# Loads of the down-weight blocks separated from their sums, in the first token group of a one-core encoder layer

## The chip, the cores and the metric

The kernel runs as one program on one core of a Trainium2 chip. The metric is the device time of one execution in microseconds (us). Before the change the median of 3 runs is 2419.88 us (2419.79 to 2422.89). The core's engines are called as in the profile: PE multiplies matrices into PSUM, PEld is its weight load, DVE, ACT and POOL work element by element, SP only issues DMA transfers. Each engine takes its instructions in the order of its own queue and waits at the head of it.

## The reference

The reference computes one layer of a streaming encoder on 2048 prompt frames and 64 sample frames, 1024 wide: RMSNorm, a combined input projection, three mixers (RG-LRU, multi-scale pooling, stick-breaking attention), an output projection, and then the part that matters here, the feed-forward block:

```
h2 = rms_norm(x, lw["ffn_norm"])
ff = jax.nn.silu(h2 @ lw["w_gate"]) * (h2 @ lw["w_up"])
x = x + ff @ lw["w_down"]
```

`w_gate` and `w_up` are 1024 x 2816, `w_down` is 2816 x 1024, all in float32.

## The kernel before

The mixers take the first 990 us or so; the feed-forward block takes the rest. Its 2112 tokens are cut into three groups of 704 columns (`GT`), each group into two halves of 352 (`HT`). The 2816 hidden units are cut into 11 pairs (p = 0 to 10) of two blocks of 128. Every float32 operand is split into a rounded high part and a low rest, and three matmuls (high by high, high by low, low by high) make one product.

The gate and up projections of a pair (`gate`, `up`) are done by `seven`: a 2 x 2 block product made of seven products instead of eight, from sums of weight blocks and sums of token blocks. One product is 12 matmuls into one of five PSUM banks called `gu`; DVE combines the banks (L1185 makes `u`, L1213 and L1236 add for the gate and the up half, L1237 multiplies gate by up), and a bank is free when its last reader is done.

In the first group the sums of gate and up weights are made on DVE (L1130, L1131, L1132, L1137), used, and written to DRAM (`wsc`) for the two groups after it. The down projection of the first group is plain: `DN(p)` loads four blocks of `w_dn` (L1271), splits them, and makes 16 results of 6 matmuls, each in one of three PSUM banks called `dn`; DVE adds each to the accumulator `acc` (L1285), which frees its bank.

Two side jobs run in the first group, for the later groups. `H2_sums` makes the token sums of the next group from `x1all` (L1154 loads, L1155 to L1161 compute, L1163 stores to `hsc`); it runs in pairs 1, 3, 5 and 7. `D_sums(p)` loads the four blocks of pair p's down weights (L1292, two transfers of 512 KB), makes four sums of them on DVE (L1294 to L1297, each 128 x 512, in place) and stores them to DRAM (`wsd`, L1299). Both jobs share two staging buffers, `xh` and `xg`, one of each, handed out in turn by `hstage()`. So a load into a staging buffer waits until the stores of the job before it have landed, and it waits at the head of SP's queue, with the other loads and stores behind it.

Where L1294 to L1297 work: the two loads fill `st[0]` and `st[1]`; L1294 reads and writes `st[1]` alone, L1295 and L1296 read both. In most pairs `st[0]` is `xh` and `st[1]` is `xg`.

What sets the order: the kernel is written as one program, but a scheduler of the framework places each engine's instructions before the launch, from its own estimate of when each will be ready (`schedule_with_timeline_sim=True`), and where two are ready it takes the one that is written earlier. So the side jobs stand in the queues where their buffers and data are expected to be ready, not where they are written. In the kernel before, all 11 `D_sums` stand within the work of the first five pairs of the first group.

Of the kernel before, what the change touches and what calls it, by code (L numbers as in the profile page):

```python
# [31 lines left out]
NF = FF // P  # L32
# [17 lines left out]
def hybrid_layer(ctx: ExitStack, tc: tile.TileContext, x_all, x_t, w_in, w_out, w_gu, w_dn, par, gates, poolw,  # L50
# [161 lines left out]
    def stage():  # L212
        return ws.tile([P, 1024], F32, name="stg", tag="stg", bufs=prm("b_st", 2))
# [752 lines left out]
    for k in range(KD):  # L966
        st = stage()
# [82 lines left out]
    def H2_row(gi):  # L1050
        rb = pr2.tile([P, GT], F32, name="rb2")
        sp.dma_start(rb, x1row[0:1, gi * GT:(gi + 1) * GT].to_broadcast([P, GT]))
        return rb
# [46 lines left out]
    def ps_gu():  # L1100
        return psF.tile([P, 512], F32, name="gu", tag="gu", bufs=5)
# [44 lines left out]
    def hstage():  # L1146
        flop[0] ^= 1
        return pr2.tile([P, 2, GT], F32, name="xh") if flop[0] else pf.tile([P, 2, GT], F32, name="xg")

    def H2_sums(gi, k, rb):  # L1150

        xh, tt = hstage(), hstage().rearrange("p a t -> p (a t)").rearrange("p (b t) -> p b t", b=4)
        for e in range(2):
            sp.dma_start(xh[:, e, :], x1all[k + 4 * e][:, gi * GT:(gi + 1) * GT])  # L1154
            dve.scalar_tensor_tensor(xh[:, e, :], xh[:, e, :], gn2_sb[:, k + 4 * e:k + 4 * e + 1], rb, ALU.mult, ALU.mult)  # L1155
        b11, b12, b21, b22 = xh[:, 0, :HT], xh[:, 0, HT:], xh[:, 1, :HT], xh[:, 1, HT:]
        t1, t2, t3, t4 = (tt[:, i, :] for i in range(4))
        dve.tensor_tensor(t1, b12, b11, ALU.subtract)
        dve.tensor_tensor(t3, b22, b12, ALU.subtract)
        dve.tensor_tensor(t2, b22, t1, ALU.subtract)  # L1160
        dve.tensor_tensor(t4, b21, t2, ALU.subtract)  # L1161
        for n, t in (("b11", b11), ("b21", b21), ("b22", b22), ("t1", t1), ("t2", t2), ("t3", t3), ("t4", t4)):
            sp.dma_start(hsc[gi][n][:, k, :], t)  # L1163

    def H2_load(gi, n, hl=None):
        st = hstage().rearrange("p a t -> p (a t)").rearrange("p (k t) -> p k t", k=4)
        sp.dma_start(st, hsc[gi][n])
        h, l = HB[n] if hl is None else hl
        act.copy(h, st)
        (gp if BL.index(n) % 2 else dve).tensor_tensor(l, st, h, ALU.subtract)  # L1170
# [37 lines left out]
    def gate(gi, p):  # L1208
        s = [pf.tile([P, GT], F32, name="s", bufs=4) for _ in range(2)]

        def use(i, x, y):
            o = s[i // 2][:, (i % 2) * HT:(i % 2) * HT + HT]
            dve.tensor_tensor(o, x, y, ALU.add)  # L1213
            act.activation(o, o, AF.Silu)

        seven(wsum(gi, p, 0), use)
        return s

    def up(gi, p, s):
        res = []  # L1220
        if gi:
            tt = pb.tile([P, 4, HT], F32, name="tt", bufs=1)
            t1, t2, t3, t4 = (tt[:, i, :] for i in range(4))
            b11, b12, b21, b22 = s[0][:, :HT], s[0][:, HT:], s[1][:, :HT], s[1][:, HT:]
        else:
            for e in range(2):
                res.append((pg.tile([P, GT], F32R, name="ah", bufs=2), pg.tile([P, GT], F32R, name="al", bufs=2)))

        def keep(b, t):
            sp.dma_start(asc[gi][p][b], t)  # L1230

        def use(i, x, y):
            cs = slice((i % 2) * HT, (i % 2) * HT + HT)
            o = s[i // 2][:, cs]
            v = tmp("v", 2)
            dve.tensor_tensor(v, x, y, ALU.add)  # L1236
            dve.tensor_tensor(o, o, v, ALU.mult)  # L1237
            if gi == 0:
                ah, al = res[i // 2]
                act.copy(ah[:, cs], o)  # L1240
                dve.tensor_tensor(al[:, cs], o, ah[:, cs], ALU.subtract)  # L1241
            elif i == 0:
                keep("b11", b11)
            elif i == 3:
                keep("b22", b22)
            elif i == 1:
                dve.tensor_tensor(t1, b12, b11, ALU.subtract)
                dve.tensor_tensor(t2, b22, t1, ALU.subtract)
                dve.tensor_tensor(t3, b22, b12, ALU.subtract)
                for b, t in (("t2", t2), ("t1", t1), ("t3", t3)):  # L1250
                    keep(b, t)
            else:
                dve.tensor_tensor(t4, b21, t2, ALU.subtract)
                keep("b21", b21)
                keep("t4", t4)

        seven(wsum(gi, p, 1), use)
        acts[p] = res
# [6 lines left out]
    def DN(p, extra=()):  # L1265
        extra = list(extra)
        for half in range(2):
            w = pg.tile([P, 2, 1024], F32R, name="wd", bufs=2)
            for q in range(2):
                r = raw()  # L1270
                sp.dma_start(r, w_dn[(2 * p + q) * P:(2 * p + q + 1) * P, half * 512:half * 512 + 512])  # L1271
                qs = slice(q * 512, q * 512 + 512)
                act.copy(w[:, 0, qs], r)
                rest(w[:, 1, qs], w[:, 0, qs], r)
            w = w.rearrange("p s (q e) -> p s q e", q=2)
            for d in range(4 * half, 4 * half + 4):
                if extra:
                    extra.pop(0)()
                cs = slice((d % 4) * P, (d % 4) * P + P)
                for (a, b) in ((0, HT), (HT, GT)):  # L1280
                    ps = psF.tile([P, 512], F32, name="dn", tag="dn", bufs=3)
                    for q in range(2):
                        ah, al = acts[p][q]
                        mm3(ps[:, :HT], w[:, 0, q, cs], w[:, 1, q, cs], ah[:, a:b], al[:, a:b], q == 0, q == 1)
                    dve.tensor_tensor(acc[:, d, a:b], ps[:, :HT], acc[:, d, a:b], ALU.add)  # L1285
                if p == NF // 2 - 1:
                    sp.dma_start(y[d][:, :GT], acc[:, d, :])
    def D_sums(p):

        st = [hstage().rearrange("p a t -> p (a t)")[:, :1024].rearrange("p (q e) -> p q e", q=2) for _ in range(2)]  # L1290
        for half in range(2):
            sp.dma_start(st[half], w_dn[2 * p * P:(2 * p + 2) * P, half * 512:half * 512 + 512].rearrange("(q p) e -> p q e", p=P))  # L1292
        a11, a12, a21, a22 = st[0][:, 0], st[0][:, 1], st[1][:, 0], st[1][:, 1]
        dve.tensor_tensor(a22, a21, a22, ALU.add)  # L1294
        dve.tensor_tensor(a21, a11, a21, ALU.subtract)  # L1295
        dve.tensor_tensor(a11, a22, a11, ALU.subtract)  # L1296
        dve.tensor_tensor(a12, a12, a11, ALU.subtract)  # L1297
        for i, t in enumerate((a11, a22, a21, a12)):
            sp.dma_start(wsd[p][:, i, :], t)  # L1299

    for p in range(NF // 2):
        s = gate(0, p)
        while pend:
            pend.pop(0)(ps_gu(), pr2)
        if p:
            DN(p - 1)
        up(0, p, s)
        if p == 0:
            sp.dma_start(acc, x1all[:, :, :GT].rearrange("k p t -> p k t"))
        if p in (1, 3, 5, 7):  # L1310
            if p == 1:
                rb2 = H2_row(1)
            H2_sums(1, p // 2, rb2)
        D_sums(p)
    DN(NF // 2 - 1, [lambda n=n: H2_load(1, n) for n in BL])
    s_g0.close()

# [11 lines left out]
    for gi in (1, 2):  # L1331
        for p in range(NF // 2):
            s = gate(gi, p)
            up(gi, p, s)
            if gi == 1:
                if p in (1, 3, 5, 7):
                    if p == 1:
                        rb2 = H2_row(2)
                    H2_sums(2, p // 2, rb2)
                if p == 8:  # L1340
                    for n in BL[:3]:
                        H2_load(2, n, HB2[n])
                if p == NF // 2 - 1:
                    HB.update(HB2)
                    for n in BL[3:]:
                        H2_load(2, n)
# [163 lines left out]
```

## Time and profile before

| what | value |
|---|---|
| median of 3 runs | 2419.88 us |
| profiled execution | 2420.12 us |
| its span, first to last instruction | 2418.3 us |
| PE busy | 2282.5 us (94%) |
| DVE busy | 1564.8 us (65%) |
| ACT, POOL busy | 984.6 us (41%), 1120.0 us (46%) |
| DMA queue's packets | 63.7% of 16 engines' span |
| mean granted TensorE clock | 0.969 |

A row of a timeline has the start in us from the span's start, the duration, the engine (SPq is SP's DMA queue), the line, the operation, output and input tiles, how many instructions are merged, and in brackets the engine's idle time before it and what ended that. A row of waits has the engine and line that waited, what released it, the total in us, how often, and the longest. Rows of windows have the busy time and instruction count of each engine, the granted clock (1.00 is full speed), the share of DMA engine time, and GB/s.

### The profile page before, as it was taken

Reading aid. Unit: us, or ns where it says so; the run is one execution under the profiler, and the core shown is the slowest. Engines: PE = TensorE matmul, PEld = TensorE weight load, DVE = VectorE, ACT = ScalarE, POOL = GpSimd, SP = SyncE. Lnnn points to the kernel's source line nnn. Section 1 sums busy time; section 2 is a strip of 40 time slices with the busy share of each in tenths; the row PEclk is TensorE's granted clock in tenths of the full one; section 3 lists DMA queues with packets and bytes.
Section 4 is the critical chain, followed back from the end, with each engine's and each line's share of the span. In section 5 each row is a group of like instructions: output and inputs, shape, how many; then the busy total and the mean of one; then the engine's idle time right before and its main releaser. Section 6 shows DMA issues by size and latency. Waiting matters only on the chain.

```text
span 2418.3 us, 38959 instructions
## 1 busy us (share of the span) xinstructions
PE 2282.5 (94%) x13966; PEld 2170.3 (90%) x13966; DVE 1564.8 (65%) x2371; ACT 984.6 (41%) x1790; POOL 1120.0 (46%) x807
## 2 busy tenths in 40 slices
PE   6988999999989989988899999999999999999999
PEld 5886878779779989888899999999999999999999
DVE  4568485795798643587767767776556665544554
ACT  4535364464565422332233334244444434333332
POOL 3534031130131133564556658487677677744442
PEclk8999999999999989999999999999999999999999
DMA  8986777666545354677764435976656666665664
GB/s 273 265 282 204 229 219 225 196 200 197 179 155 160 104 151 124 230 242 250 241 212 117 141 114 185 298 237 185 190 181 195 196 189 207 185 184 157 213 213 141
DMA packets 288260, 475.65 MB, mean 197 GB/s; under 512 B 44226, under 2 KB 153603, under 8 KB 280131
## 3 DMA queue, kind: packets, MB, share of 16 engines
q1 hardware_dynamic: 288066, 473.16, 63.7%
q8 instruction: 111, 1.82, 0.3%
q14 instruction: 83, 0.67, 0.1%
HBM read 337.22 MB, written 135.82 MB: 196 GB/s over the span
## 4 chain that ended last, share of the span: by engine, by line
PE 64%; DVE 14%; DMA 14%; issue 3%; ACT 2%; SPq 1%; POOL 1%; DVEq 0%; ACTq 0%; POOLq 0%
PE gu L78 37%; PE mm L78 13%; PE dn L78 10%; PE z L78 2%; PE av L78 2%; DVE C L665 2%; DMA x<-in_w_gu 1%; PE tp L709 1%; DVE xc L537 1%; DMA rbk<-row 1%; DMA rb<-xrow 1%; DVE s L1237 1%; DMA K<-kscr 1%; DMA xg<-in_w_dn 1%; DMA x1all<-xr 1%
## 5 line engine op out<-in xcount | busy, mean ns | idle before, releaser
L86 POOL TENSOR_TENSOR w<-x,w 128x512 fp32r<-128x512 f32 x539 | 773.5, 1448 | 525.6 <-ACT w L1108 482.3
L78 PE MATMUL gu<-ht,w 128*128 128x352 f32 x2131 | 543.3, 326 | 14.6 <-ACT w L1108 5.7
L1108 ACT CAST w<-x 128x512 fp32r<-128x512 f32 x539 | 328.0, 618 | 415.5 <-PE gu L78 261.6
L78 PE MATMUL mm<-hTh,w 128*128 128x512 f32 (+3 forms) x1632 | 433.1, 343 | 13.8 <-DVE xr L1009 8.5
L78 PE MATMUL gu<-hb,w 128*128 128x352 f32 x1622 | 407.1, 324 | 7.3 <-ACT w L1108 4.6
L78 PEld LDWEIGHTS gu<-ht,w 128*128 128x128 f32 x2131 | 379.6, 190 | 17.8 <-ACT w L1108 9.1
L78 PE MATMUL gu<-lt,w 128*128 128x352 f32 x1163 | 356.9, 325 | 0.0
L78 PEld LDWEIGHTS mm<-hTh,w 128*128 128x128 f32 x1632 | 292.0, 195 | 43.7 <-DVE xr L1009 9.5
L78 PEld LDWEIGHTS gu<-hb,w 128*128 128x128 f32 x1622 | 286.3, 189 | 9.0 <-ACT w L1108 5.4
L78 PE MATMUL mm<-hTl,w 128*128 128x512 f32 (+3 forms) x816 | 278.8, 342 | 1.4 <-POOL hTl L307 1.0
L78 PE MATMUL gu<-lb,w 128*128 128x352 f32 x991 | 279.3, 324 | 0.0
L78 PE MATMUL dn<-ah,wd 128*128 128x352 f32 x704 | 193.6, 333 | 26.1 <-DVE acc L1285 23.1
L78 PEld LDWEIGHTS gu<-lt,w 128*128 128x128 f32 x1163 | 217.5, 190 | 0.0
L78 PEld LDWEIGHTS gu<-lb,w 128*128 128x128 f32 x991 | 180.6, 190 | 0.0
L78 PEld LDWEIGHTS mm<-hTl,w 128*128 128x128 f32 x816 | 158.7, 195 | 16.1 <-POOL hTl L307 1.4
L665 DVE TENSOR_TENSOR_SCAN C<-z,C,zero 128x512 f32<-128x512 f32 (+4 forms) x148 | 160.5, 1087 | 13.2 <-ACT z L657 6.7
L78 PEld LDWEIGHTS dn<-ah,wd 128*128 128x128 f32 x704 | 130.2, 195 | 29.7 <-DVE acc L1285 26.0
L1237 DVE TENSOR_TENSOR s<-s,v 128x352 f32<-128x352 f32 x132 | 143.2, 1087 | 2.5
L1185 DVE TENSOR_TENSOR u<-gu,u 128x352 f32<-128x352 f32 x132 | 68.6, 520 | 81.1 <-PE gu L78 80.0
L78 PE MATMUL z<-K,q 128*128 128x512 f32 (+4 forms) x328 | 102.5, 396 | 18.3 <-DVE C L665 8.4
L574 POOL TENSOR_TENSOR i<-i,xc 128x512 f32<-128x512 f32 (+1 forms) x16 | 27.3, 1709 | 198.1 <-ACT i L562 146.9
L78 PE MATMUL dn<-al,wd 128*128 128x352 f32 x352 | 116.8, 332 | 0.4 <-DVE al L1241 0.4
(318 smaller groups left out, 4284.5 us busy)
## 6 DMA issues: line engine op xcount, KB each, us to landing
x<-in_w_gu SPq DMA_DIRECT2D x220, 256.0 KB, 3.9
w<-wk SPq DMA_DIRECT2D x46, 1024.0 KB, 6.1
x<-wsc SPq DMA_DIRECT2D x176, 256.0 KB, 4.1
wsc<-x SPq DMA_DIRECT2D x88, 256.0 KB, 3.9
x<-in_w_dn SPq DMA_DIRECT2D x77, 256.0 KB, 3.9
wk<-w SPq DMA_DIRECT2D x16, 1024.0 KB, 9.4
x<-wsd SPq DMA_DIRECT2D x44, 256.0 KB, 4.0
V<-vscr SPq DMA_DIRECT2D x40, 256.0 KB, 3.9
```

The source lines that it names most:

```text
L78: pe.matmul(out, lhsT, rhs, start=start, stop=stop)
L86: gp.tensor_tensor(out, src, hi, ALU.subtract)
L537: dve.scalar_tensor_tensor(xc[:, a:b], xa[:, s + j:s + j + b - a], pv("cw", c * 4 + j), xc[:, a:b], ALU.mult, ALU.add)
L574: gp.tensor_tensor(i, i, xc, ALU.mult)
L665: dve.tensor_tensor_scan(C[:n, :w][:, ::-1], om[:n, :w][:, ::-1], zero1[:n].to_broadcast([n, w]), carry, ALU.mult, ALU.add)
L709: pe.transpose(tp[:, kt, :], at[:, kt * P:(kt + 1) * P], ident)
L1108: act.copy(w[:, 0, :], src)
L1185: add = lambda o, x, y: dve.tensor_tensor(o, x, y, ALU.add)
L1237: dve.tensor_tensor(o, o, v, ALU.mult)
```

## The change

`D_sums` is cut in two. `D_load(p)` takes the two staging buffers and issues the two loads; `D_sums()` makes the sums and stores of the pair that was loaded last. In the first group `D_load(p)` stands at the end of pair p, and its sums at the end of pair p + 1, ahead of `H2_sums` and of the next `D_load`. The load of the last pair (p = 10) stands after the last `DN` with its loads of token sums, and its sums after `up` of the first pair of the second group. Nothing that is computed changes. In the changed program the loads are L1294, the four sums L1301 to L1304, the stores L1306.

```diff
+    dst_ = []
+
+    def D_load(p):
         st = [hstage()... for _ in range(2)]
         for half in range(2):
             sp.dma_start(st[half], w_dn[...])
+        dst_.append((p, st))
+
+    def D_sums():
+        p, st = dst_.pop(0)
         a11, a12, a21, a22 = st[0][:, 0], st[0][:, 1], st[1][:, 0], st[1][:, 1]
...
+        if p:
+            D_sums()
         if p in (1, 3, 5, 7):
             if p == 1:
                 rb2 = H2_row(1)
             H2_sums(1, p // 2, rb2)
-        D_sums(p)
+        if p < NF // 2 - 1:
+            D_load(p)
     DN(NF // 2 - 1, [lambda n=n: H2_load(1, n) for n in BL])
     s_g0.close()
+    D_load(NF // 2 - 1)
...
             up(gi, p, s)
             if gi == 1:
+                if p == 0:
+                    D_sums()
```

First place, SP's queue, around the load of pair 2 (`wsd_130` is the scratch of pair 0, so `wsd_131` and `wsd_132` are those of pairs 1 and 2; `wsc` stores and L1116 loads belong to gate and up weights). Before:

```order
L1292 DMA xg<-in_w_dn 128x2x512
L1141 DMA wsc_1_111<-x_10883 128x512
L1299 DMA wsd_131<-xh 128x512
L1141 DMA wsc_1_111<-x_10881 128x512
L1299 DMA wsd_132<-xg 128x512
L1292 DMA xh<-in_w_dn 128x2x512
L1141 DMA wsc_1_111<-x_10887 128x512
L1116 DMA x_11076<-in_w_gu 128x512
```

And now:

```order
L1306 DMA wsd_131<-xg 128x512
L1141 DMA wsc_1_111<-x_10875 128x512
L1306 DMA wsd_131<-xh 128x512
L1141 DMA wsc_1_111<-x_10873 128x512
L1294 DMA xg<-in_w_dn 128x2x512
L1294 DMA xh<-in_w_dn 128x2x512
L1141 DMA wsc_1_111<-x_10879 128x512
L1116 DMA x_11068<-in_w_gu 128x512
L1306 DMA wsd_132<-xg 128x512
```

The two loads of pair 2 now stand together; before, the second stood behind a store of pair 2's own first sum, and that sum waits for the first load. The second of the two stores of pair 1 out of `xg` now stands nearer to the first load.

Second place, DVE's queue, around the sums of pair 7, at the end of the down projection and in the up projection of pair 3. Before:

```order
L1185 TENSOR_TENSOR u_11927<-gu,u_11894 128x352
L1185 TENSOR_TENSOR u_11894<-gu,u_11894 128x352
L1236 TENSOR_TENSOR v<-gu,u_11927 128x352
L1285 TENSOR_TENSOR acc<-dn,acc 128x352
L1237 TENSOR_TENSOR s<-s,v 128x352
L1285 TENSOR_TENSOR acc<-dn,acc 128x352
L1294 TENSOR_TENSOR xg<-xg 128x512
L1285 TENSOR_TENSOR acc<-dn,acc 128x352
L1295 TENSOR_TENSOR xg<-xh,xg 128x512
```

And now:

```order
L1185 TENSOR_TENSOR u_11919<-gu,u_11886 128x352
L1285 TENSOR_TENSOR acc<-dn,acc 128x352
L1301 TENSOR_TENSOR xg<-xg 128x512
L1285 TENSOR_TENSOR acc<-dn,acc 128x352
L1302 TENSOR_TENSOR xg<-xh,xg 128x512
L1285 TENSOR_TENSOR acc<-dn,acc 128x352
L1185 TENSOR_TENSOR u_11886<-gu,u_11886 128x352
L1236 TENSOR_TENSOR v<-gu,u_11919 128x352
L1303 TENSOR_TENSOR xh<-xg,xh 128x512
```

The first sum of pair 7 now stands ahead of the second L1185 and of the first L1236 of that up projection; before it stood behind both.

Third place, DVE's queue, in the last down projection of the first group and the first pair of the second. Before:

```order
L1170 TENSOR_TENSOR lt_9625<-xh,ht_9624 128x1408
L1285 TENSOR_TENSOR acc<-dn,acc 128x352 x3
L1155 SCALAR_TENSOR_TENSOR xg<-xg,gn_sb,rb_16087 128x704
L1213 TENSOR_TENSOR s<-gu,c_15550 128x352
L1155 SCALAR_TENSOR_TENSOR xg<-xg,gn_sb,rb_16087 128x704
L1158 TENSOR_TENSOR xh<-xg 128x352
L1185 TENSOR_TENSOR u_15582<-gu,u_15552 128x352
```

And now:

```order
L1170 TENSOR_TENSOR lt_9625<-xh,ht_9624 128x1408
L1285 TENSOR_TENSOR acc<-dn,acc 128x352 x3
L1213 TENSOR_TENSOR s<-gu,c_15542 128x352
L1301 TENSOR_TENSOR xh<-xh 128x512
L1185 TENSOR_TENSOR u_15574<-gu,u_15544 128x352
L1302 TENSOR_TENSOR xg<-xh,xg 128x512
L1285 TENSOR_TENSOR acc<-dn,acc 128x352
L1303 TENSOR_TENSOR xg<-xh,xg 128x512
L1285 TENSOR_TENSOR acc<-dn,acc 128x352
L1304 TENSOR_TENSOR xg<-xg 128x512
```

The sums of pair 10 stand here now; the token sums of the third group (L1155 onward), which stood here, come about a dozen rows later. Elsewhere the sums of pairs 0 to 9 stand within a few rows of where they stood, still within the first five pairs of the first group: those of pair 6 three rows earlier (ahead of an L1132, an L1213 and an L1185), those of pair 9 ahead of the first L1285 of their down projection instead of behind it.

## Rows read from the trace of the kernel before

**Rows 1.** Windows of the first group: PE, PEld, DVE, ACT, POOL, clock, DMA, GB/s.
```profile
1060.00:1240.00 180.00, 154.91 (x898) 151.72 (x897) 133.98 (x215) 50.93 (x97) 90.44 (x65) 0.92 0.76 246
1240.00:1420.00 180.00, 180.00 (x1128) 180.00 (x1128) 127.80 (x199) 62.26 (x121) 109.23 (x78) 1.00 0.45 132
1100.00:1120.00 20.00, 13.21 (x59) 12.46 (x58) 12.99 (x22) 4.75 (x10) 7.41 (x7) 0.74 0.74 240
1220.00:1240.00 20.00, 20.00 (x121) 20.00 (x120) 15.46 (x27) 5.60 (x10) 9.43 (x7) 0.95 0.77 237
```

**Rows 2.** Waits from 1060 to 1240 us: who waited, for whom, total, times, longest.
```profile
PE dn L78 <- DVE acc L1285: 22.9, 7, 5.6
DVE xg L1294 <- DMA xg<-in_w_dn: 19.1, 6, 5.5
DVE xg L1295 <- DMA xh<-in_w_dn: 8.1, 5, 2.4
```

**Rows 3.** Timeline of PE: its gaps in that stretch.
```profile
1066.71 0.43 PE L78 MATMUL dn<-ah,wd 128*128 128x352 f32 x1 [2.31 <-DVE acc L1285]
1086.67 0.40 PE L78 MATMUL gu<-hb,w 128*128 128x352 f32 x1 [1.74 <-DVE v L1236]
1106.17 0.66 PE L78 MATMUL dn<-ah,wd 128*128 128x352 f32 x1 [4.87 <-DVE acc L1285]
1110.52 0.66 PE L78 MATMUL dn<-ah,wd 128*128 128x352 f32 x1 [1.93 <-DVE acc L1285]
1160.61 0.66 PE L78 MATMUL dn<-ah,wd 128*128 128x352 f32 x1 [5.57 <-DVE acc L1285]
1175.58 0.43 PE L78 MATMUL dn<-ah,wd 128*128 128x352 f32 x1 [2.19 <-DVE acc L1285]
1196.49 0.40 PE L78 MATMUL gu<-ht,w 128*128 128x352 f32 x1 [0.34 <-DVE v L1236]
1211.41 0.43 PE L78 MATMUL dn<-ah,wd 128*128 128x352 f32 x1 [3.77 <-DVE acc L1285]
1215.85 0.66 PE L78 MATMUL dn<-ah,wd 128*128 128x352 f32 x1 [2.29 <-DVE acc L1285]
```

**Rows 4.** Lines L1292 and L1299: from issue to landing, in that order.
```profile
DMA to landing us min/median/max: 3.5/5.8/7.8
...
DMA to landing us min/median/max: 2.4/4.0/10.9
```

**Rows 5.** Timeline of SP and DVE at the sums of pair 2.
```profile
1059.51 0.38 SPq L1292 DMA_DIRECT2D xh<-in_w_dn  x1
...
1058.17 0.71 DVE L1294 TENSOR_TENSOR xg<-xg 128x512 f32<-128x512 f32 x1 [3.12 <-DMA xg<-in_w_dn]
1065.06 1.16 DVE L1295 TENSOR_TENSOR xg<-xh,xg 128x512 f32<-128x512 f32 x1 [1.75 <-DMA xh<-in_w_dn]
```

**Rows 6.** Timeline of DVE at the sums of pair 6.
```profile
1151.40 1.72 DVE L1294 TENSOR_TENSOR xg<-xg 128x512 f32<-128x512 f32 x1 [2.54 <-DMA xg<-in_w_dn]
1156.27 1.16 DVE L1295 TENSOR_TENSOR xg<-xh,xg 128x512 f32<-128x512 f32 x1 [0.28 <-DMA xh<-in_w_dn]
```

**Rows 7.** Timeline of DVE and PE at the sums of pair 7.
```profile
1180.50 1.15 DVE L1185 TENSOR_TENSOR u<-gu,u 128x352 f32<-128x352 f32 x2
1189.26 1.52 DVE L1294 TENSOR_TENSOR xg<-xg 128x512 f32<-128x512 f32 x1 [5.54 <-DMA xg<-in_w_dn]
...
1192.16 0.32 PE L78 MATMUL gu<-hb,w 128*128 128x352 f32 x1
```

**Rows 8.** Timeline of DVE at the sums of pair 9.
```profile
1214.67 0.69 DVE L1294 TENSOR_TENSOR xg<-xg 128x512 f32<-128x512 f32 x1 [3.32 <-DMA xg<-in_w_dn]
```

**Rows 9.** Timeline of DVE where the second group begins.
```profile
1505.71 1.89 DVE L1170 TENSOR_TENSOR lt<-xh,ht 128x1408 fp32r<-128x1408 f32 x1 [0.30 <-ACT ht L1169]
1513.44 0.51 DVE L1185 TENSOR_TENSOR u<-gu,u 128x352 f32<-128x352 f32 x1
1524.36 0.95 DVE L1155 SCALAR_TENSOR_TENSOR xg<-xg,gn_sb,rb 128x704 f32<-128x704 f32 x1 [3.11 <-DMA xg<-x1all]
```

More of the change, by code (lines that the diff above doesn't have):

```diff
@@ L1287, in DN @@
                     sp.dma_start(y[d][:, :GT], acc[:, d, :])
-    def D_sums(p):
+    dst_ = []
+    def D_load(p):
         st = [hstage().rearrange("p a t -> p (a t)")[:, :1024].rearrange("p (q e) -> p q e", q=2) for _ in range(2)]
```

## The prediction

> **What bounds the kernel now.** I read the windows first. From 1240 to 1420 us, where the first group runs without its side jobs, PE is busy all of the time at full clock: 1128 matmuls in 180 us, 0.1596 us each [rows 1]. From 1060 to 1240 us, with the side jobs between, it issues 898 in the same time [rows 1]. At 0.1596 us these would take 143.3 us, so 36.7 us are lost there: 25.1 us are gaps (180 less 154.91), and 11.6 us are matmuls at the lower clock (154.91 less 143.3), which the granted clock of 0.92 shows too. This stretch is what the change can move.
>
> The waits say what ends the gaps: 22.9 us of PE's stand behind DVE's addition to `acc`, L1285 [rows 2]. DVE is not full there (133.98 of 180 us, rows 1); it stands itself, 19.1 us at L1294 and 8.1 us at L1295, until a load of down weights has landed [rows 2]. A load takes 5.8 us from issue to landing, a store 4.0 us [rows 4]. So PE waits for an addition that is queued behind a sum that waits for a load. Nine gaps make up the 25 us [rows 3]. After the gaps of 4.87 and 5.57 us the first matmul takes 0.66 us, after those of 2.31 and 2.19 us 0.43 us [rows 3]: the long ones cost clock as well. In the stretch of 20 us with the gaps of 4.87 and 1.93 us only 59 matmuls were issued [rows 1], worth 9.4 us, so that 10.6 us went.
>
> **What the change does to the queues.** It would take these waits away if the sums stood a pair later than their load. They do not: the scheduler puts an instruction where it expects it to be ready, and the order of the changed kernel shows the sums of pairs 0 to 9 again within a few rows of their old places, each soon behind its load. Nothing is removed: 11 times two loads, four sums and four stores before and after. What is left are shifted rows. Up to pair 1 the queues are the same, so these 36.7 us begin alike.
>
> The Trainium skill's page "DMA: Bandwidth & Descriptors", section Rules for kernel authors, says to issue a DMA early, compute, and wait on its semaphore late, so that the fixed cost overlaps. That is the rule by which this change would win. The order says that the wait is not late here, so I keep the rule for a rival.
>
> *Pair 2.* Before, its second load stood behind a store of its own first sum: issued at 1059.51, awaited by L1295 until 1065.06 us [rows 5]. Now both loads stand together. The first also waits for a store of pair 1 that now stands later. The waits of 3.12 and 1.75 us [rows 5] become one, which I put between 3.12 and 4.87 us. PE's gap of 2.31 us stands behind the second wait [rows 3, 5]. I take 1.5 us off. Low end: that gap and the next of 1.74 us are both gone, 4.05 us. High end: the gap doubles, 2.3 us more. The value is nearer to the gap it removes.
>
> *Pairs 3 to 5.* Loads and sums stand in the old order by up to two rows: nothing, and covered as before.
>
> *Pair 6.* Its first sum waits until 1151.40 us [rows 6]. It moves ahead of an L1132, an L1213 and an L1185, some 0.7, 0.5 and 0.5 us (as the 0.71 us of a 128 x 512 sum in rows 5, and a little under half of the 1.15 us of two L1185 in rows 7). With the same landing these 1.7 us come behind the wait, and the 0.28 us that DVE waited at L1295 [rows 6] absorb little. The first addition of that down projection, which ends the gap of 5.57 us [rows 3], comes later. The load stands a few rows earlier on SP, perhaps half a microsecond. I take 1.2 us more, from 1.0 us less (load earlier by as much) to 3.0 us more (1.7 us and a second load late by 1.3 us).
>
> *Pair 7.* Here DVE waits longest, 5.54 us until 1189.26 us, and PE nearly escapes: its gap behind it is 0.34 us [rows 3, 7]. It escapes because both L1185 were done by 1181.65 us [rows 7], the L1236 next, and so the bank of the fifth product was free. Now the second L1185 and that L1236 stand behind the wait. The load is issued behind the same token-sum stores and lands as before. After it come L1301 (1.52 us), two L1285 and the L1302 (some 1.7 us), L1185 and L1236 (1.0 us): the bank is free at about 1193.5 us. Five banks let PE do four products first; the one that takes this bank began at 1192.16 us [rows 7]. That is 1.3 us late, and the next two banks are read by L1236 rows that are now later too, for which I add 1.2 us: 2.5 us more. Low end nothing; high end the whole old wait, 5.5 us. I stay near the 1.3 us that the rows give.
>
> *Pair 9.* The sum that waits 3.32 us [rows 8] moves ahead of the first L1285, so the gap of 3.77 us grows by up to 3.3 us and the second, 2.29 us [rows 3], goes, because two additions then follow at once; the load stands two rows earlier (some 0.8 us). Together 0.2 us more; ends 2.3 us less and 3.3 us more.
>
> *Pair 10.* Its sums leave this stretch. From 1220 to 1240 us PE was busy all the time [rows 1], so nothing comes back; at most the 1.0 us that the clock of 0.95 means there.
>
> They go to the start of the second group. The first sum needs `xh`, whose load waits at SP's head until L1170 has read the buffer, 1507.60 us [rows 9]; with 5.8 us [rows 4] it lands at 1513.4. The L1185 behind it stood at 1513.44 us [rows 9] and comes 0.7 us later. The token sums follow only when the stores have landed; they were waited for 3.11 us at 1524.36 [rows 9]. Behind the waiting load on SP stand weight loads of the second group, covered by the blocks already loaded; behind L1301 on DVE stand L1285 rows and `u`, covered by three and five banks. I take 1.0 us more, from nothing to 5 us (a wait of 5.8 us with little cover).
>
> The sum: -1.5 + 1.2 + 2.5 + 0.2 + 0 + 1.0 = 3.4 us more. The profiled execution took 2420.12 us, so 2423.5; the median of the runs is 0.24 us lower, so **2423.3 us**. All low ends together give 8.4 us less, all high ends 19 us more.
>
> **The rivals.** *Slower:* the wait at pair 7 grows into a long gap. It decides once PE stands there for about as long as in the gap of 3.77 us, because then the clock falls too. For it: DVE now holds a bank through that whole wait. Against: 10.5 us of products lie between 1181.65 and 1192.16 us. The price is that of the stretch with the 4.87 us gap, 10.6 us: 2430.5 us.
>
> *Faster by a better start:* the joined loads of pair 2 bring the staging buffers round earlier, the loads of pairs 3 and 4 arrive in time, and the gaps of 4.87 and 1.93 us close. With pair 2's own 1.5 us that is 8.3 us: 2411.6 us. For it: the buffers are handed on in a chain. Against: PE and DVE come earlier by the same amount.
>
> *The change does what it says:* all waits at L1294 and L1295 go. Of the 36.7 us only the two gaps that other lines explain stay, 1.74 and 2.19 us: 32.8 us less, 2387 us. This is what the skill's rule on waiting late would give. Against it stands the order.
>
> **How the numbers follow.** A measurement here tells about 0.2% (4.8 us) from no change. My forecast, within that, has 0.41. Slower by pair 7 or by a like chain at pair 6 or the second group's start: 0.35. The better start: 0.19. The waits gone: 0.05. So faster 0.24, same 0.41, slower 0.35. The range reaches to both nearer rivals and a little over: 2411 to 2432 us.
>
> **What would show it.** Waits at L1301 and L1302 for loads still near 27 us between 1060 and 1240 us; the wait at pair 2 single and its gap shorter; DVE idle some 8 us ahead of pair 7's L1301 and a PE gap behind an L1185 or L1236 about 1192 us; PE gaps in that stretch again near 25 us and the matmul count near 900; a short DVE wait at L1301 about 1510 us. If those waits are gone, the forecast is wrong in its first step; if the gap at pair 7 is over 4 us or absent, in its fourth.

## The result: 0.59% slower, and the profile after

The changed kernel takes 2434.33 us (median of 7 runs, 2429.28 to 2443.94); beside it the kernel before took 2422.89 us. The ratio on record is 1.0059, with a 95% interval of 1.0043 to 1.0076 (the two medians alone give 1.0047). In a later measurement it was 2434.31 against 2416.92 us, 1.0076 (1.0061 to 1.0091). The forecast was 2423.3 us, range 2411 to 2432.

The profiled execution took 2435.69 us, 15.6 us more than that of before. Windows of the kernel after, the columns as in [rows 1]; the first two rows answer to the first two there:

```profile
1060.00:1240.00 180.00, 148.38 (x851) 143.92 (x851) 133.64 (x204) 47.21 (x90) 90.82 (x62) 0.92 0.74 238
1240.00:1420.00 180.00, 180.00 (x1129) 180.00 (x1127) 126.39 (x196) 62.25 (x119) 109.80 (x78) 1.00 0.40 121
1000.00:1260.00 260.00, 221.94 (x1292) 216.25 (x1291) 198.84 (x286) 79.95 (x152) 146.56 (x101) 0.93 0.74 238
1480.00:1660.00 180.00, 167.17 (x992) 162.52 (x991) 126.66 (x172) 67.65 (x115) 122.31 (x78) 0.97 0.78 248
```

The last two stretches of the kernel before:

```profile
1000.00:1260.00 260.00, 228.09 (x1324) 222.32 (x1323) 199.83 (x299) 81.16 (x154) 146.60 (x103) 0.93 0.76 248
1480.00:1660.00 180.00, 172.16 (x1055) 170.06 (x1054) 132.12 (x176) 71.57 (x122) 125.59 (x85) 0.99 0.77 246
```

A matmul at full clock is 0.1596 us, as before. In the first stretch 32 fewer were issued, 5.1 us; in the second 63 fewer, 10.1 us. Together that is 15.2 of the 15.6 us. Between them nothing was lost: in this pair of executions two thirds of the loss lie where the second group begins. Of the 10.1 us there, 5.0 are gaps of PE (172.16 less 167.17 us busy); the other 5.1 are matmuls at the lower clock, 0.97 against 0.99. How the loss divides is not firm: the execution traced in the later measurement issued 1283 and 1027 matmuls in the two stretches, 41 and 28 fewer than this execution of before, 6.5 and 4.5 us.

In the crowded stretch the waits are still there, which answers to [rows 2]. Waits of the kernel after, 1060 to 1240 us:

```profile
PE dn L78 <- DVE acc L1285: 26.0, 11, 8.8
DVE xg L1301 <- DMA xg<-in_w_dn: 18.0, 7, 5.1
DVE xg L1302 <- DMA xh<-in_w_dn: 5.9, 4, 2.6
PE gu L78 <- DVE v L1236: 4.2, 3, 2.2
DVE xg L1301 <- DMA x<-in_w_dn: 3.4, 1, 3.4
```

DVE stands 27.3 us at L1301 and L1302, at the sums of pairs 2 to 9. The 27.2 us of [rows 2] are not those of the same pairs. They hold 2.4 us of pair 10, and they leave out 3.12 us of pair 2, which ended before 1060 us [rows 5], and a wait of pair 3 that the profile of before puts down to issue:

```profile
DVE xg L1294 <- issue: 3.5, 1, 3.5
```

For pairs 2 to 9 it was 31.4 us before. Pair 2 lost 4.3 us of its waits; those of pairs 3 to 9 together stayed (26.5 before, 26.8 now). PE's gaps are 31.6 us (180 less 148.38) instead of 25.1. The larger of them, and one of the second group, in the timeline of PE after:

```profile
1105.81 0.43 PE L78 MATMUL dn<-ah,wd 128*128 128x352 f32 x1 [3.09 <-DVE acc L1285]
1110.31 0.66 PE L78 MATMUL dn<-ah,wd 128*128 128x352 f32 x1 [3.00 <-DVE acc L1285]
1162.93 0.66 PE L78 MATMUL dn<-ah,wd 128*128 128x352 f32 x1 [6.45 <-DVE acc L1285]
1197.85 0.40 PE L78 MATMUL gu<-ht,w 128*128 128x352 f32 x1 [0.53 <-DVE v L1236]
1201.49 0.40 PE L78 MATMUL gu<-ht,w 128*128 128x352 f32 x1 [1.47 <-ACT ah L1240]
1221.37 0.66 PE L78 MATMUL dn<-ah,wd 128*128 128x352 f32 x1 [8.80 <-DVE acc L1285]
...
1573.92 0.40 PE L78 MATMUL gu<-hb,w 128*128 128x352 f32 x1 [2.47 <-DVE s L1213]
```

DVE ahead of them, at the sums of pairs 2 (two rows), 7, 8 and 9, in the timeline of after; these answer to [rows 5, 7, 8]:

```profile
1059.00 1.32 DVE L1301 TENSOR_TENSOR xg<-xg 128x512 f32<-128x512 f32 x1 [0.38 <-DMA xg<-in_w_dn]
1062.60 1.09 DVE L1302 TENSOR_TENSOR xg<-xh,xg 128x512 f32<-128x512 f32 x1 [0.17 <-DMA xh<-in_w_dn]
...
1189.97 1.80 DVE L1301 TENSOR_TENSOR xg<-xg 128x512 f32<-128x512 f32 x1 [5.06 <-DMA xg<-in_w_dn]
...
1209.45 0.82 DVE L1302 TENSOR_TENSOR xg<-xh,xg 128x512 f32<-128x512 f32 x1 [2.61 <-DMA xh<-in_w_dn]
...
1219.27 1.61 DVE L1301 TENSOR_TENSOR xg<-xg 128x512 f32<-128x512 f32 x1 [2.08 <-DMA xg<-in_w_dn]
```

Against [rows 3], the gap at pair 9's sum is one of 8.80 us instead of 3.77 and 2.29, and the gap behind L1236 near 1197 us stayed small.

The second group's start in the timeline of DVE after; it answers to [rows 9]:

```profile
1511.29 2.26 DVE L1170 TENSOR_TENSOR lt<-xh,ht 128x1408 fp32r<-128x1408 f32 x1
...
1517.61 0.69 DVE L1301 TENSOR_TENSOR xh<-xh 128x512 f32<-128x512 f32 x1 [1.58 <-DMA xh<-in_w_dn]
...
1533.48 1.74 DVE L1155 SCALAR_TENSOR_TENSOR xg<-xg,gn_sb,rb 128x704 f32<-128x704 f32 x1 [2.76 <-DMA xg<-x1all]
...
1546.83 0.95 DVE L1155 SCALAR_TENSOR_TENSOR xg<-xg,gn_sb,rb 128x704 f32<-128x704 f32 x1 [5.01 <-issue]
...
1563.92 0.95 DVE L1155 SCALAR_TENSOR_TENSOR xg<-xg,gn_sb,rb 128x704 f32<-128x704 f32 x1 [0.58 <-DMA xg<-x1all]
...
1571.96 0.95 DVE L1155 SCALAR_TENSOR_TENSOR xg<-xg,gn_sb,rb 128x704 f32<-128x704 f32 x1 [5.67 <-DMA xg<-x1all]
...
1582.41 1.86 DVE L1155 SCALAR_TENSOR_TENSOR xg<-xg,gn_sb,rb 128x704 f32<-128x704 f32 x1 [3.55 <-issue]
...
1587.69 1.53 DVE L1155 SCALAR_TENSOR_TENSOR xg<-xg,gn_sb,rb 128x704 f32<-128x704 f32 x1
```

And the token sums there in the kernel before, the first, one that waits, and the last (the other that waits is in [rows 9]):

```profile
1508.83 0.94 DVE L1155 SCALAR_TENSOR_TENSOR xg<-xg,gn_sb,rb 128x704 f32<-128x704 f32 x1
...
1536.60 3.79 DVE L1155 SCALAR_TENSOR_TENSOR xg<-xg,gn_sb,rb 128x704 f32<-128x704 f32 x2 [2.25 <-DMA xg<-x1all]
...
1555.67 0.94 DVE L1155 SCALAR_TENSOR_TENSOR xg<-xg,gn_sb,rb 128x704 f32<-128x704 f32 x1
```

Pair 10's own wait is short, 1.58 us. What follows it is not: the first token sum for the third group comes 24.65 us later than before and the last 32.0 us later. With the lag of 5.1 us taken off, the chain starts 19.6 us late, and its waits, 5.4 us before, are 17.6 us now. They stand in front of L1213, L1236 and L1185, which free the `gu` banks: behind these three lines PE's gaps from 1540 to 1660 us sum to 9.9 us, and to 4.4 before. While pair 10's blocks themselves were summed and stored, from 1512 to 1551 us, PE has no gap of over 0.1 us. SP's queue after shows how long the buffers were held, from the second load of pair 10 to the first loads of the token sums, which land for the sum at 1533.48:

```profile
1513.58 0.38 SPq L1294 DMA_DIRECT2D xh<-in_w_dn  x1
...
1528.74 0.80 SPq L1154 DMA_DIRECT2D xg<-x1all  x2
```

### The profile page after: what moved, and what is told of

It reads as the page before. It is cut to its first block, busy times and chain, and to the rows that moved or that the text cites. A ratio compares the mean times of both kernels' runs of the same rounds, so it can differ in the third digit from the quotient of the medians.

```text
span 2433.8 us, 38954 instructions
## 1 busy us (share of the span) xinstructions
PE 2289.3 (94%) x13966; PEld 2174.0 (89%) x13966; DVE 1572.2 (65%) x2371; ACT 984.4 (40%) x1790; POOL 1126.1 (46%) x807
## 4 chain that ended last, share of the span: by engine, by line
PE 65%; DVE 14%; DMA 13%; issue 3%; ACT 2%; POOL 1%; SPq 1%; DVEq 0%; ACTq 0%; POOLq 0%
PE gu L78 36%; PE mm L78 14%; PE dn L78 9%; PE z L78 2%; DVE C L665 2%; PE av L78 1%; PE tp L709 1%; DMA xg<-in_w_dn 1%; DMA rbk<-row 1%; DMA x1all<-xr 1%; DVE s L1237 1%; POOL w L86 1%; DMA x<-in_w_gu 1%; DMA wsd<-xh 1%; PE tp L78 1%
## 5 line engine op out<-in xcount | busy, mean ns | idle before, releaser
L78 PEld LDWEIGHTS gu<-ht,w 128*128 128x128 f32 x2131 | 377.7, 189 | 24.0 <-ACT w L1108 10.1
L574 POOL TENSOR_TENSOR i<-i,xc 128x512 f32<-128x512 f32 (+1 forms) x16 | 27.4, 1710 | 204.2 <-ACT i L562 139.6
L1185 DVE TENSOR_TENSOR u<-gu,u 128x352 f32<-128x352 f32 x132 | 68.6, 520 | 78.7 <-PE gu L78 77.7
```

Source lines behind the costliest of these rows:

```text
L78: pe.matmul(out, lhsT, rhs, start=start, stop=stop)
L574: gp.tensor_tensor(i, i, xc, ALU.mult)
L1185: add = lambda o, x, y: dve.tensor_tensor(o, x, y, ALU.add)
```

## Experiments

Each kernel was timed beside the kernel before on the same chip, and only ratios of one chip are compared, since the median of before was 2416.9 to 2422.9 us from one measurement to the next.

**Is it pair 10 or the split?** First the split alone:

```diff
-        if p < NF // 2 - 1:
-            D_load(p)
+        D_load(p)
+    D_sums()
     DN(NF // 2 - 1, [lambda n=n: H2_load(1, n) for n in BL])
     s_g0.close()
-    D_load(NF // 2 - 1)
...
             if gi == 1:
-                if p == 0:
-                    D_sums()
```

> The changed kernel, but the last pair's blocks are loaded and summed ahead of DN(10) in the first group, as in the kernel before; the split of pairs 0 to 9 stays. Theory A (the 10 us that the second group's start lost came from pair 10's sums, which now stand ahead of the token sums of the third group in the chain of staging buffers): the lag stays at the +6.0 us that the trace shows from 1260 to 1470 us, or a little less as DN(10) has its old neighbours, so 2425 to 2430 us, and the waits of the token sums L1155 near 1533 to 1582 us (2.76, 5.01, 5.67, 3.55 us) fall back to the 3.1 and 2.3 us of before. Theory B (the second group's loss is the first group's lag arriving out of step, and pair 10 is innocent): no change, 2432 to 2436 us, with the long L1155 waits still there.

Measured: 2422.84 us, ratio 1.0021 (1.0008 to 1.0034), with waits of 6.6 us at the token sums. Then pair 10 alone, the other pairs as before (`if p < NF // 2 - 1: D_load(p); D_sums()` in the first group, pair 10 as in the change):

> The kernel before, with one part of the change: pair 10's blocks are loaded after DN(10) and summed in the second group's first pair; pairs 0 to 9 are loaded and summed together as before. Theory A: the first group ends within 2 us of before and the second group's start costs about 10 us, 2429 to 2434 us. Theory B (the cost is the split in the first group): within 2 us of before, 2421 to 2425 us.

Measured: 2424.48 us, 1.0025 (1.0007 to 1.0043). The ranges of both runs had been set from a before of 2422.89 us; here before was 2418.05 us. Taken as differences from before, the split (4.8 us) lies in A's range and pair 10 (6.4 us) at the lower edge of A's and outside B's. Both parts cost, by theory A's direction; pair 10 less than the 10 us expected. In the trace of pair 10 alone 36 matmuls are missing from 1480 to 1660 us, 5.7 us. Then the change with pair 10 behind the token sums (load in pair 7 of the second group, sums written in pair 8):

> The changed kernel, but pair 10's blocks are loaded behind the last token sums of the second group (pair 7) and summed in pair 8; pairs 0 to 9 as in the changed kernel. Theory A, in the smaller size that the kernel with pair 10 alone moved showed (+6 us over before on one chip): pair 10 costs because it stands ahead of the third group's token sums in the chain of staging buffers, so behind them it costs nothing, and what stays is the split of pairs 0 to 9, which was +5 us with pair 10 put back: 2420 to 2426 us where before is 2418, and the waits at L1155 near 1530 to 1585 us fall from 17 us to under 8. Theory B (pair 10's sums cost wherever they stand in the second group): 2429 to 2436 us.

Measured: 2426.34 us, 1.0038 (1.0026 to 1.0050), 0.3 us over the upper edge of A. The token sums are back at 1504.47 us with waits of 4.1 us, but the scheduler let pair 10's sums run ahead to 1567.74 us, where they waited 5.66 us for their load, as DVE's timeline shows:

```profile
1567.74 0.69 DVE L1301 TENSOR_TENSOR xh<-xh 128x512 f32<-128x512 f32 x1 [5.66 <-DMA xh<-in_w_dn]
```

In this trace 34 matmuls are missing from 1480 to 1660 us, 5.4 us: in the staging buffers pair 10 cost behind the token sums too.

**Is it the staging buffers or the work?** Pair 10 at the same place in the program, in buffers of its own, beside the changed kernel:

```diff
+    def D_load_own(p):
+        tt = pb.tile([P, 4, HT], F32, name="tt", bufs=1)...
+        xs = [pb.tile([P, 2, HT], F32, name="xa", bufs=3)... for _ in range(2)]
+        st = [tt[:, :512], tt[:, 512:1024], xs[0][:, :512], xs[1][:, :512]]
+        for i in range(4):
+            sp.dma_start(st[i], w_dn[...])
...
-    D_load(NF // 2 - 1)
+    D_load_own(NF // 2 - 1)
```

> The changed kernel with pair 10's four blocks in buffers of their own (the tiles tt and xa of the later stages, free at that time) instead of the two staging buffers; everything else as in the changed kernel. Theory A (pair 10 costs because it occupies the staging buffers that the third group's token sums need next): the token sums go back to about 1505 to 1556 us, their waits fall from 17.6 to under 8 us, and what is left is the split: ratio to before 1.001 to 1.003, 2419 to 2425 us where before is 2418. Theory H (the cost is the load, the four sums and the four stores of pair 10 at that place, whatever buffers they use): ratio 1.005 to 1.007, 2429 to 2435 us.

> The changed kernel itself, on the same chip as the kernel with pair 10's own buffers, to set the two side by side: 1.005 to 1.007 of before by all theories.

Measured: 2422.14 us, 1.0021 (1.0008 to 1.0035), with its own buffers; 2434.31 us, 1.0076, without. With its own buffers the kernel stands where the split alone stood (1.0021), so pair 10 cost nothing measurable when it did not hold `xh` and `xg` (its loads are four of 256 KB instead of two of 512). That is theory A's number, and the waits of the token sums fell to 5.3 us. But the run moves two things at once: the scheduler put these sums behind three of the four pairs of token sums, at 1557.15 us, where the changed kernel has them at 1517.61 us, ahead of all. Two observations speak against H and for the buffers. PE had no gap while the sums ran at the early place (above). And the run before this one, with pair 10 in the staging buffers at 1567.74 us, issued 1021 matmuls from 1480 to 1660 us where this one issued 1072 (the intervals of the two ratios overlap). No run has its own buffers at the early place. DVE with own buffers, first token sum, first sum of pair 10, last but one token sum:

```profile
1514.86 0.94 DVE L1155 SCALAR_TENSOR_TENSOR xg<-xg,gn_sb,rb 128x704 f32<-128x704 f32 x1
...
1557.15 0.68 DVE L1311 TENSOR_TENSOR xa<-xa 128x512 f32<-128x512 f32 x1
...
1563.07 1.95 DVE L1155 SCALAR_TENSOR_TENSOR xg<-xg,gn_sb,rb 128x704 f32<-128x704 f32 x1 [1.22 <-DMA xg<-x1all]
```

The windows of 1540 to 1640 us, with own buffers:

```profile
1540.00:1640.00 100.00, 97.98 (x611) 97.46 (x610) 79.62 (x101) 41.23 (x73) 76.36 (x52) 1.00 0.86 285
```

and in the changed kernel beside it:

```profile
1540.00:1640.00 100.00, 93.50 (x565) 91.39 (x564) 67.62 (x97) 38.37 (x69) 68.39 (x47) 0.98 0.84 275
```

46 matmuls, 7.3 us of the 10.1 us between these two executions (2423.98 and 2434.04 us), lie in these 100 us. The Trainium skill's page "Perfetto Trace Analysis", section Optimization Strategy, says that consistent bubbles can mean that there is no SBUF or PSUM for the next tile. This pair of kernels is such a case, with the bubbles one step removed, on PE behind DVE: in these 100 us PE's gaps are 6.5 us with the two staging buffers and 2.0 with the others.

**What does the split cost by itself?** The control (before, pair 10 in pair 2 of the third group), and the same with the split:

> The kernel before with pair 10 alone loaded and summed in pair 2 of the third group, nothing paced: the control. Pair 10's sums ran ahead to 1226 us and hid there, so taking them away gives 0 to 3 us, and five VectorE microseconds in the third group, where PE is busy all the time, cost under 2 us: 2414 to 2420 us by both theories. If it is under 2412, the gain of the paced kernels is from pair 10 and not from the pacing.

> The changed kernel, not paced, with pair 10 loaded and summed in pair 2 of the third group: the split of pairs 0 to 9 by itself, with nothing of pair 10 in the first or second group. If the change's cost is the sum of two parts (split about +5 us, pair 10 ahead of the third group's token sums about +6 to +9), this is 2419 to 2425 us where before is 2418 and the control with pair 10 alone in the third group was 2416. If the split costs nothing by itself and only sharpens what pair 10 does, 2414 to 2418 us.

Measured: 2416.16 us, 0.9993 (0.9983 to 1.0003), and 2422.36 us, 1.0023 (1.0007 to 1.0038). Then pair 9 too out of the first group, with and without the split:

> The changed kernel, not paced, with pairs 9 and 10 loaded and summed in pairs 2 and 5 of the third group: the split of pairs 0 to 8. Theory J (the split costs through pair 9's sums, whose first stands ahead of the first acc addition of DN(3) and makes the stall of 8.5 to 8.8 us seen in all four kernels with the unpaced split): that stall is gone, the waits of PE for acc fall from 26 us to under 20, and the time is that of the same kernel without the split within 2 us. Rival K (the split moves all sums against the banks a little, and the stall at DN(3) only collects it): still 3 to 6 us over the kernel without the split, 2418 to 2423 us.

> The kernel before, not paced, with pairs 9 and 10 loaded and summed in pairs 2 and 5 of the third group: the partner of the kernel with the split. Two pairs fewer in the crowded stretch from 1060 to 1260 us, of which pair 10's was worth 0 to 2 us: 2410 to 2417 us where before is 2418, with the waits of PE for acc at 15 to 22 us (22.9 before). If pair 9's sums cost nothing there: 2415 to 2418 us.

Measured: 2421.74 us, 1.0016 (1.0006 to 1.0027), with the split, 2414.48 us, 0.9995 (0.9982 to 1.0007), without. So the split costs 5 to 7 us: 0.21% against before, 0.30% and 0.21% between partners. Theory J falls: without pair 9 the longest gap is 6.8 instead of 8.8 us and PE's waits for `acc` are 22.7 us, but the cost stays, as K has it. Windows 1000 to 1260 us, pair 10 in the third group, together:

```profile
1000.00:1260.00 260.00, 229.12 (x1342) 223.71 (x1341) 194.57 (x298) 82.09 (x156) 147.47 (x103) 0.93 0.75 241
```

and split:

```profile
1000.00:1260.00 260.00, 221.85 (x1285) 215.96 (x1285) 198.74 (x288) 79.51 (x151) 144.56 (x99) 0.93 0.72 232
```

57 matmuls fewer, 9.1 us in these two executions. Which of the pairs' shifts makes them stays open.

**Does it pay to let the sums really wait?** One edge of issue order puts each pair's sums behind the last DVE instruction of `up(0, p)`:

```diff
         if p:
-            D_sums()
+            with behind("dve"):
+                D_sums()
```

> The changed kernel with one edge of issue order for each pair of the first group: VectorE issues the sums of the pair before only behind the last instruction of up(0, p) that it was given, so the scheduler can no longer put them among the last acc additions of DN(p-1) or ahead of the v additions. No wait is added, only an order. Theory C (the split did not pay because the sums still run ahead and their waits for a load or a staging buffer stand in front of instructions that free PSUM banks): the waits at L1301 and L1302 (25 us) move behind the bank-freeing additions, the stalls of PE at dn<-acc (26.0 us from 1060 to 1300 us) fall under 10, the first group is 15 to 30 us shorter, and with the second group's start unchanged the time is 2400 to 2420 us. Rival D (the sums cost what their 5 us of VectorE cost wherever they stand, or a later store of them delays the next staging buffer as much): within 5 us of the changed kernel, 2429 to 2439 us.

The same edge on the kernel before, around `D_sums(p)`:

> The kernel before with the same edge: load and sums of a pair still stand together in the program, but VectorE issues the sums behind the last instruction of up(0, p). Theory C: the order on VectorE is what counts and the split is not, since SyncE issues the loads freely as soon as a staging buffer is free; 2385 to 2410 us, that is 8 to 15 us under the paced kernel with the split, by the second group's start. If the split has a worth of its own once the sums are paced, the gap between this kernel and the paced split is under 5 us. Rival D: within 5 us of before, 2418 to 2428 us.

Measured: 2433.24 us, 1.0060 (1.0041 to 1.0079), and 2427.92 us, 1.0043 (1.0030 to 1.0055). Both times lie in D's ranges, but the traces show part of C's gain in the first stretch and, behind it, a loss that neither theory had. Windows of the paced split:

```profile
1000.00:1260.00 260.00, 246.95 (x1501) 241.89 (x1500) 201.12 (x291) 88.49 (x171) 162.05 (x113) 0.99 0.59 183
1260.00:1480.00 220.00, 208.34 (x1278) 206.80 (x1276) 169.38 (x253) 69.72 (x135) 128.80 (x88) 0.98 0.59 184
1480.00:1660.00 180.00, 155.04 (x883) 151.81 (x884) 112.29 (x155) 64.58 (x108) 108.63 (x70) 0.92 0.78 253
```

Against before, the first stretch issued 177 matmuls more, 28 us, as theory C has it, though PE's waits for `acc` from 1060 to 1300 us fell to 14.0 us and not under 10. Sums spread over the group press less, 183 GB/s instead of 248, and no wait of a sum for its load is left between 1000 and 1480 us. But the next stretches issued 102 and 172 fewer (before: 1380 and 1055), 44 us. The last addition to `acc` and the first sum of a pair of hidden blocks (tile `tt`, the "t-block" of the expectations below) show where. A row here has the shortest, median and longest duration in ns and the first and last start; the paced split:

```profile
L1285 DVE TENSOR_TENSOR acc<-dn,acc x176: 504/524/527, 1043.2 to 1497.6; 128x352 f32<-128x352 f32 x176
...
L1247 DVE TENSOR_TENSOR tt<-s x6: 509/524/1501, 1555.7 to 1695.8; 128x352 f32<-128x352 f32 x6
```

and before:

```profile
L1285 DVE TENSOR_TENSOR acc<-dn,acc x176: 505/518/527, 1044.6 to 1533.0; 128x352 f32<-128x352 f32 x176
...
L1247 DVE TENSOR_TENSOR tt<-s x6: 524/526/1499, 1549.3 to 1683.7; 128x352 f32<-128x352 f32 x6
```

DN(10) ends 35.4 us sooner, yet the second group comes 6.4 us later. The token blocks of that group pass through the same two buffers, now behind the sums of pair 9, whose last store was issued at 1490.27 us. ACT waits for them in the paced split:

```profile
1495.28 1.37 ACT L1169 CAST ht<-xg 128x1408 fp32r<-128x1408 f32 x1 [12.98 <-DMA xg<-hsc1t]
1502.28 1.36 ACT L1169 CAST hb<-xh 128x1408 fp32r<-128x1408 f32 x1 [5.62 <-DMA xh<-hsc1b]
```

So the next step was to pace and to take the last pairs to the third group (`if gi == 2 and p == ...: D_load(q); D_sums()`), first pair 10:

> The paced kernel with load and sums together, with pair 10 loaded and summed in pair 2 of the third group. Theory E: pacing gave 14 us of PE time between 1000 and 1260 us (241.8 against 228.1 us busy in the kernel before) and lost it at the second group's start, where pair 10's sums at 1489 us stand ahead of the second group's token blocks in the chain of staging buffers (PE waits 14.3 us for hb and ht, ACT 21 us for hsc1). With pair 10 gone from there those waits fall under 6 us and the gain stays: 2398 to 2412 us. Rival F: the token blocks are late because pacing moved every pair's sums later, not by pair 10's; the waits for hb and ht stay over 8 us and the time is 2418 to 2428 us.

> The same with the split: pairs 0 to 9 loaded one pair before their sums and the sums paced, pair 10 in the third group. Theory E: 2400 to 2415 us; pair 9's sums now stand behind up(0, 10), beside DN(10) and the second group's token blocks, so it is slower than the paced kernel without the split by 3 to 10 us. Rival F: 2423 to 2435 us. If the split has a worth of its own when the sums really wait a pair, it is faster than the paced kernel without it by over 3 us.

Measured: 2412.38 us, 0.9977 (0.9966 to 0.9988), and 2432.28 us, 1.0049 (1.0032 to 1.0065). E holds for the first but for 0.4 us over its upper edge, and PE's waits for hb and ht are gone. It failed for the split, which lies in F's range; its pair 9 is summed at 1490.25 us, behind `up(0, 10)`, and takes the place of pair 10 ahead of the token blocks; ACT's longest wait for them is 13.20 us. Then the last two or three pairs:

> The split with paced sums, pairs 9 and 10 loaded and summed in pairs 2 and 5 of the third group. With pair 9 still in the first group DN(10) ended at 1504.6 us (before: 1533) and yet the first t-block of the second group came at 1559.0 us (before: 1549.3), as pair 9's sums at 1490 us stood ahead of the token blocks in the chain of staging buffers (waits for hsc1: 22 us). Theory E: with the last sums at about 1450 us the token blocks start near 1470 us as before, the waits for hb and ht (15.7 us) fall under 5, and 15 to 30 us of the 28 us by which DN(10) ended sooner stay: 2390 to 2405 us where before is 2418. Rival G: the first group's end is set by the token blocks whatever stands ahead of them, and what pacing gives it is lost again: 2412 to 2424 us.

> Load and sums together and paced, pairs 9 and 10 in pairs 2 and 5 of the third group. Theory E: the last sums are at 1408 us, the waits for hsc1 (12 us with pair 9 in the first group) go under 4, and the time is 4 to 12 us under the 2412 of the kernel with pair 10 alone in the third group: 2400 to 2409 us. Rival G: 2410 to 2418 us.

> The split with paced sums, pairs 8, 9 and 10 in pairs 1, 4 and 7 of the third group. Theory E: the last sums are at about 1406 us, as in the paced kernel without the split and without pairs 9 and 10, so within 4 us of that one: 2395 to 2409 us. If the split has a worth of its own, more than 4 us under it. Rival G: 2410 to 2424 us. If the sums crowd the third group, its PE (busy 200 of 200 us from 1900 to 2100 us in the kernel before) shows gaps of over 5 us there.

Measured: 2411.92 us, 0.9973 (0.9957 to 0.9988); 2409.11 us, 0.9971 (0.9957 to 0.9985); 2407.47 us, 0.9956 (0.9939 to 0.9973). Moving pair 9 brings the paced split down from 1.0049 to 0.9973, some 18 us, though not to E's 2390 to 2405: it lies between the ranges of E and G. Of the other two the first is 0.1 us over E's range, the second in it. With as many sums out of the way, split and together are equal within their intervals: these runs show no worth of the split by itself. The last has the lowest ratio here, 0.44% under before; its interval overlaps those of the other two. Its windows:

```profile
1000.00:1260.00 260.00, 247.41 (x1497) 243.20 (x1496) 202.31 (x292) 86.63 (x168) 161.10 (x111) 0.98 0.59 182
1260.00:1480.00 220.00, 209.37 (x1286) 208.22 (x1285) 167.69 (x249) 77.65 (x142) 135.86 (x89) 0.98 0.59 187
1480.00:1660.00 180.00, 172.76 (x1062) 170.93 (x1061) 126.05 (x170) 69.41 (x123) 121.72 (x86) 0.99 0.76 243
```

173 matmuls more than before, then 94 fewer, then 7 more: 86, or 13.7 us, against 9.9 us between the medians. The three pairs are summed where the third group begins, from 1821.97 to 1863.34 us, and DVE waits for their loads there. The first of these sums:

```profile
1821.97 1.80 DVE L1301 TENSOR_TENSOR xg<-xg 128x512 f32<-128x512 f32 x1 [5.54 <-DMA xg<-in_w_dn]
```

The window around it, before:

```profile
1660.00:1900.00 240.00, 236.17 (x1461) 235.83 (x1460) 144.69 (x193) 102.33 (x181) 174.71 (x125) 0.99 0.62 189
```

and with the three pairs:

```profile
1660.00:1900.00 240.00, 234.20 (x1444) 233.07 (x1444) 152.42 (x207) 98.39 (x174) 170.50 (x121) 0.99 0.67 211
```

17 matmuls fewer: the third group takes back about 2.7 us. The 200 us from 1900 to 2100 us, which the expectation named, hold none of these sums, and PE is busy all the time there.

## Why the prediction was wrong

*The step that failed is the last term of the sum*, "They go to the start of the second group ... I take 1.0 us more, from nothing to 5 us". It measured 10.1 us in the trace (63 matmuls), 5.7 us in the trace with pair 10 alone, 4.5 us in the second trace of the changed kernel, and 12 us between the medians of the changed kernel and the one with pair 10 in its own buffers: the size is not firm, but all of these are over four times the 1.0 us, and all but one lie outside its 0 to 5. I priced one wait, of L1301 for its load, and that came short, as said: 1.58 us at 1517.61 us. I wrote that the token sums follow only when the stores have landed, and then did not follow that chain. Load 5.8, sums 4.4 (measured, 1517.61 to 1522.06), store 4.0 [rows 4], and the next load: that is a turn of the buffers of about 20 us, which I could have added up. In the trace it took 19.9 us, from the load's issue at 1513.58 to the first token sum at 1533.48. Before, two of the four pairs of token sums began within 17 us, beside DN(10); now the second begins behind its last addition (1540.9 us), so that three stand beside gate and up alone, where a wait on DVE holds a `gu` bank.

*The other terms of the first group* were too small in sum, +2.4 forecast and 5.1 us measured by the matmuls, 5 to 7 us by the runs.

- The change does not do what it says: right, 27.3 us of waits at the sums of pairs 2 to 9, against 31.4 before. That rival, 2387 us, is out for this kernel. The paced split does what it says, and is not faster either: the Trainium skill's rule in "DMA: Bandwidth & Descriptors", section Rules for kernel authors (issue early, wait late), held for its waits, all gone, and not for the time.
- Pair 2, -1.5: the two waits fell from 4.87 to 0.55 us, more than thought, but PE's gap of 2.31 became four that sum to 2.15.
- Pairs 3 to 5, 0: the gaps of 4.87 and 1.93 became 3.09 and 3.00, 0.7 less, that of 1.74 became 2.22, and there are new ones of 0.58 and 1.43 us at 1128.97 and 1143.14 us. In all 1.8 us more.
- Pair 6, +1.2: the gap went from 5.57 to 6.45, 0.9 more. Right.
- Pair 7, +2.5: DVE waited 5.06 us ahead of L1301, but the bank came only 0.53 us late; another 1.47 us came behind ACT. 1.7 us more, in its range, but mostly not by the bank that it was worked out from: in part luck. The sign of a wait of some 8 us ahead of that sum did not come.
- Pair 9, +0.2: the sum did move ahead of the first L1285 and the second gap went, but the first grew by 5.0 us, not 3.3. 2.7 us more, over ten times the value and still in its range. Ahead of it pair 8's L1302 had waited 2.61 us, so DVE came late.
- The removal of pair 10 from the stretch, 0: the control with pair 10 in the third group was 0.07% under before, within its interval. Right.
- PE's gaps near 25 us and a count near 900 did not come: 31.6 us and 851.

The slower rival had its place at pair 7, or "a like chain at pair 6 or the second group's start". It happened at the last of these, by a chain of buffers and not by one long gap: from 1512 us on single gaps are at most 2.47 us. The granted clock fell behind them all the same, to 0.91 from 1560 to 1580 us (1.00 before). That the rival's price, 10.6 us, is near what was measured is luck: it is the price of another stretch.

## What to carry to other kernels

When a job is moved past others that use the same few buffers, price the whole turn (load, work, store, next load) and follow it to the last user, not the first wait. Loads and sums that were written apart did not run apart here, because a scheduler ordered them; read the order, and pin it. A stall that was removed paid only as far as the next user of the buffers was early too: 28 us gained in one stretch were 44 us lost in the next two until the last pairs were taken out of the way.

## What was not expected of the hardware

In the paced split PE's granted clock was 0.92 from 1480 to 1660 us (0.99 before), where ACT had waited 12.98 and 5.62 us for token blocks. The 172 matmuls that are missing there are 27.4 us, while PE's gaps grew by 17.1 us (155.04 busy against 172.16). The other 10.3 us are the lower clock: here a late block cost more than the gap it left.

DMA gave more than the crowded stretch of before used: 285 GB/s from 1540 to 1640 us with pair 10 in its own buffers, with PE 97.98 of 100 us busy, against 246 GB/s in [rows 1]. So 246 GB/s was not the most that DMA moved in this program; the transfers of the two stretches are not the same.
